# Hybrid decoder step: convolution tails transposed four chunks at a time, diagonal products regrouped by rows, sample scores of two batches together

## Chip, cores and metric

The kernel runs on one core of one Trainium2 chip. The metric is the device time of one execution in microseconds. Before the change the median of three runs is 1380.89 us (1379.9 to 1382.13).

## What is computed

One inference step of one decoder layer, for 256 prompt tokens and 8 sample requests of 4 tokens each (288 columns in all), in float32:

```python
proj = rmsnorm(x) @ w_in                       # -> z, xbc, dt, q, k, v
xbc, conv_new = causal_conv(xbc, conv0)        # width 4; conv_new = last 3 inputs per request
y, ssm_new = ssd_scan(x, dt, a, B, C, h0)      # per head: y_diag = (C B^T * decay) @ x, plus the state's part
x = x + concat(gated rmsnorm(y), sliding-window attention) @ w_out
x = x + cross_attn(rmsnorm(x), memory keys and values) # 4 heads of 128, 256 memory tokens per request
x = x + ffn(rmsnorm(x))                        # 5632 hidden units
```

The outputs are the two token streams after a last norm and all new states and caches. Among them are `conv_new` for the prompt (3 rows of 1536 channels) and for the 8 sample requests (8 times 3 rows).

## The kernel before

**Layout.** All activations stand transposed: channels on the 128 partitions, the 288 tokens along the free axis. A weight matrix is read in chunks of 128 x 1024 numbers into `raw` (3 buffers). ScalarE rounds a chunk to `hi` (line 159) and VectorE subtracts to get `lo` (line 79, called from 160 on), with 4 buffers of each; TensorE then makes three products per tile, `lo x`, `hi x` and `hi x_lo` (lines 169 to 171, named `mm`). A chunk is 24 such products of 288 columns.

**Order of the work.** The program is written as projections that follow each other. Small work is put in between by `later(n, fn)`: a heap holds functions that are emitted n chunk steps later. A scheduler then sorts the instructions of each engine by priority and by its own estimate of when an operand is ready, and each engine runs its list in that order; waits are semaphores. Weight loads have the highest priority. SyncE (SP) issues nearly all transfers.

**Convolution tails.** `conv_pair` handles two 128-channel chunks: it scales the projection (`xr`), makes four taps and the silu, and copies the last 3 prompt columns and the last 3 columns of each sample request into a tile `cc` of 27 columns. Four steps later `emit` transposes the two `cc` tiles on TensorE (two products with the identity, line 118), copies the 27 x 256 result to `co`, and SP sends two output transfers (lines 723 and 724). There are 12 chunks, so 6 pairs.

**Diagonal products.** `ssd(jj)` handles four heads. `diag` makes for each pair j of heads one PSUM tile: for the three token blocks c (128, 128 and 32 rows) and the two heads, a product of 64 output partitions (line 823). The blocks c = 0, 1 contract over 128 rows, c = 2 over 32 rows. There are four calls, jj = 0 to 3.

**Natural B.** `bc_products` transposes the B chunks (`nat_transpose`, six transposes), VectorE and ScalarE copy them out (line 745), and TensorE makes the B-C products (line 771).

**Sample scores.** In cross-attention, `sample_keys(b)` loads the keys of request b and transposes them (8 transposes), and `score` makes four products, one per head, each in its own 32 output partitions of one PSUM tile (line 1162). All eight requests accumulate into the same tile, since `qm` is zero outside the columns of its own request.

Of the kernel before, what the change touches and what calls it, by code (L numbers as in the profile page):

```python
# [8 lines left out]
F32 = mybir.dt.float32  # L9
# [3 lines left out]
ALU = mybir.AluOpType  # L13
AX = mybir.AxisListType

P = 128
D = 2048
KC = D // P
TP = 256
TS = 32  # L20
T = TP + TS
NB = 8
# [24 lines left out]
def tile_hymba_step(ctx: ExitStack, tc: tile.TileContext, I: dict, O: list, stop: int = 99):  # L47
    nc = tc.nc
# [3 lines left out]
    def tl(pool, shape, dt, tag):  # L52
        uid[0] += 1
        return pool.tile(shape, dt, name=f"{tag}_{uid[0]}", tag=tag)
# [17 lines left out]
    def psum(tag="ps"):  # L72
        return tl(p_ps, [P, 512], F32, "ps")
# [7 lines left out]
    def stt(out, in0, s, in1, op0, op1):  # L81
        nc.vector.scalar_tensor_tensor(out=out, in0=in0, scalar=s, in1=in1, op0=op0, op1=op1)  # L82
# [32 lines left out]
    def transpose(out, in_):  # L115
        k = in_.shape[0]
        b = in_.base_partition() if callable(in_.base_partition) else in_.base_partition
        nc.tensor.transpose(out, in_, ident[b:b + k, 0:k])  # L118
# [6 lines left out]
    def later(n, fn):  # L125
        uid[0] += 1
        heapq.heappush(pend, (clock[0] + n, uid[0], fn))
# [109 lines left out]
    for j, nm_ in enumerate(("sinks", "dt_bias", "a_log")):  # L237
# [4 lines left out]
    sinkb, dtb, aexp, sinkc, dsk, nsinkb, nsinkc = (  # L242
        hvec[:, a:b] for a, b in ((0, 16), (16, 32), (32, 48), (48, 50), (50, 58), (58, 74), (74, 76)))
# [78 lines left out]
    def ts(w=T, n=P, dt=F32):  # L322
        return tl(mxs, [P, 320], dt, "s")[:n, :w]
# [366 lines left out]
    conv_state()  # L690
    RW = 3 + TP + 56

    def conv_pair(c0, pcs):
        ccs = []
        for j in range(2):
            c, pc = c0 + j, pcs[j]
            xr, ac = ts(RW), ts(RW)
            smp = lambda t_: t_[:, 259:315].rearrange("p (b s) -> p b s", s=7)
            nc.gpsimd.memset(xr[:, 0:3], 0.0)
            nc.scalar.copy(smp(xr)[:, :, 0:3], scT[:, c].rearrange("p (b k) -> p b k", k=3))  # L700
            tt(nc.vector, xr[:, 3:259], pc[:, :TP], rstdb[:, :TP], ALU.mult)
            tt(nc.vector, smp(xr)[:, :, 3:7], pc[:, TP:T].rearrange("p (b t) -> p b t", t=4),
               rstdb[:, TP:T].rearrange("p (b t) -> p b t", t=4), ALU.mult)
            n = RW - 3
            act(ac[:, :n], xr[:, 0:n], AF.Identity, scale=cwT[:, c:c + 1], bias=nwcol(V_CB, c))
            for k in range(1, 4):
                stt(ac[:, :n], xr[:, k:k + n], cwT[:, 12 * k + c:12 * k + c + 1], ac[:, :n], ALU.mult, ALU.add)
            nc.gpsimd.memset(ac[:, n:], 0.0)
            act(xc[c][:, :TP], ac[:, :TP], AF.Silu)
            act(xc[c][:, TP:T].rearrange("p (b t) -> p b t", t=4), smp(ac)[:, :, 0:4], AF.Silu)  # L710
            cc = tl(mxr, [P, 27], F32, "cc")
            nc.scalar.copy(cc[:, 0:3], xr[:, 256:259])
            nc.scalar.copy(cc[:, 3:27].rearrange("p (b k) -> p b k", k=3), smp(xr)[:, :, 4:7])
            ccs.append(cc)

        def emit():
            pt = psum()
            for j in range(2):
                transpose(pt[:27, j * P:(j + 1) * P], ccs[j])
            co = ts(256)  # L720
            nc.scalar.copy(co[:27], pt[:27, 0:256])
            cs_ = slice(c0 * P, c0 * P + 256)
            nc.sync.dma_start(o_pconv[0, 0, :, cs_], co[0:3])
            nc.sync.dma_start(o_sconv[0].rearrange("b k c -> (b k) c")[:, cs_], co[3:27])

        later(4, emit)

    CH = ((0, P), (P, TP), (TP, T))
    hv_ = lambda t_: t_.rearrange("p (h d) -> p h d", d=64)
# [80 lines left out]
    def ssd(jj):  # L810
        g = jj // 2
        sgv = sgs[jj]
        *xnat, xe, xe0, xe1, xes = nat_transpose(2 * jj, 4 * jj)

        def diag():
            for j in range(2):
                i = 2 * jj + j
                ps = psum()
                for c in range(3):
                    a, b_ = CH[c]  # L820
                    for hf in range(2):
                        h4 = 2 * j + hf
                        nc.tensor.matmul(ps[64 * hf:64 * hf + 64, a:b_], xnat[c][:, 64 * h4:64 * h4 + 64],  # L823
                                         sgv[c][:, h4], start=True, stop=True)
                stt(xc[i], xc[i], dsk[:, i:i + 1], ps[:, :T], ALU.mult, ALU.add)
            x3_ = ts(256, 96, F32R)
            nc.scalar.copy(x3_[0:32], xes)
            nc.scalar.copy(x3_[64:96], xes)
            tt(nc.vector, x3_[32:64], xes, f32(x3_[0:32]), ALU.subtract)
            xs3[jj] = x3_  # L830
            later(2, states)

        def states():
            ps = psum()
            nc.tensor.matmul(ps[:, 0:256], bnat[0][:, g * P:(g + 1) * P], xe, start=True, stop=True)
            st0 = ts(256)
            nc.scalar.copy(st0, ps[:, 0:256])
            ps = psum()
            for j in range(2):
                for c, x_ in ((0, xe0), (1, xe1)):  # L840
                    nc.tensor.matmul(ps[:, j * P:(j + 1) * P], x_[:, j * P:(j + 1) * P],
                                     bnat[c][:, g * P:(g + 1) * P], start=(c == 0), stop=(c == 1))
            so = ts(256)
            nc.scalar.copy(so, ps[:, 0:256])
            nc.sync.dma_start(o_pssm[0, 0].rearrange("(k i f) p n -> k (f p) i n", k=4, f=2)[jj],
                                so.rearrange("p (i n) -> p i n", n=P))
            later(1, lambda: inter(st0))

        def inter(st0):
            ps = psum()  # L850
            for j in range(2):
                for hf in range(2):
                    h4 = 2 * j + hf
                    nc.tensor.matmul(ps[64 * hf:64 * hf + 64, j * P:(j + 1) * P], st0[:, 64 * h4:64 * h4 + 64],
                                     xc[10 + g][:, P:TP], start=True, stop=True)
            yo = ts(256)
            for j in range(2):
                i = 2 * jj + j
                tt(nc.vector, yo[:, j * P:(j + 1) * P], ps[:, j * P:(j + 1) * P], ecs[i][:, 0:P], ALU.mult)
                tt(nc.vector, xc[i][:, P:TP], xc[i][:, P:TP], yo[:, j * P:(j + 1) * P], ALU.add)  # L860
            part_done(g)

        later(1, diag)


# [249 lines left out]

    cmk, cmv = I["cache_mem_k"][0], I["cache_mem_v"][0]
    pS, pO = [], []
    pm = []

    def softmax(rows):  # L1120
# [21 lines left out]
    def sample_keys(b):  # L1142
        kk = sample_load(b, cmk)
        if not pS:
            pS.append(psum())

        def trans():
            kTb = []
            for hp in range(2):
                ps = psum()  # L1150
                for j in range(2):
                    for mc in range(2):
                        transpose(ps[:, 256 * j + P * mc:256 * j + P * mc + P],
                                  kk[mc][2 * hp + j])
                    k_ = tl(p_xb, [P, T], F32, "xb")[:, :256] if b < 2 else ts(256)
                    (nc.vector.tensor_copy if hp else nc.scalar.copy)(k_, ps[:, 256 * j:256 * j + 256])
                    kTb.append(k_)
            later(max(1, t_q + 5 - clock[0]), lambda: score(kTb))

        def score(kTb):  # L1160
            for h in range(4):
                nc.tensor.matmul(pS[0][32 * h:32 * h + 32, :TP], qm[h][:, b], kTb[h], start=(b == 0),  # L1162
                                 stop=(b == NB - 1))
            if b == NB - 1:
                sx = ts(256)
                softmax([(pS[0][:, :TP], sx, tl(lr, [P, 2], F32, "st"))])
                later(2, lambda: weights(sx))

        def weights(sx):
            ps = psum()  # L1170
            for mc in range(2):
                transpose(ps[:, mc * P:(mc + 1) * P], sx[:, mc * P:(mc + 1) * P])
                for h in range(4):
                    p_ = ts(256)
                    nc.gpsimd.memset(p_, 0.0)
                    p_ = p_.rearrange("p (b t) -> p b t", b=NB)
                    v = p_.rearrange("p b (c t) -> p (b c) t", t=4)[:, 0:64:9]
                    o0 = mc * P + h * TS
                    nc.vector.tensor_copy(v, ps[:, o0:o0 + TS].rearrange("p (b t) -> p b t", t=4))
                    pm.append(p_)  # L1180
            for b2 in range(NB):
                later(b2 // 2 + 1, lambda b2=b2: values(b2))

        later(2, trans)
# [273 lines left out]
```

## Time and profile before

| what | value |
|---|---|
| median of 3 runs | 1380.89 us |
| the profiled execution, its own time | 1382.05 us |
| its span, first to last instruction | 1380.3 us |
| TensorE busy | 1367.6 us (99%) |
| VectorE / ScalarE busy | 810.5 us (59%) / 638.4 us (46%) |
| mean transfer rate | 175 GB/s |

How to read it: "busy" counts a matmul from its start to a modelled end, and matmuls overlap in the pipeline. What a product costs in a stream is therefore the distance from its start to the start of the next row, not its duration. A row of the timeline that merges several equal instructions gives the start of the first and their count. PE is TensorE, DVE is VectorE, ACT is ScalarE. `128*27 128x128` reads: stationary operand of 128 rows and 27 columns, moving operand of 128 partitions and 128 columns.

### The profile page before, as it was taken

What the parts mean: (1) busy time and instruction counts of PE and PEld (TensorE: products, weight loads), DVE (VectorE), ACT (ScalarE), POOL (GpSimd) and SP (SyncE); (2) the same over time, 40 slices, a digit from 0 to 9 for tenths busy, and PEclk for the clock granted to TensorE, in tenths of its full rate; (3) what the DMA queues carried; (4) which work ended last, traced back from release to release, by engine and by line L of the source; (5) the groups of instructions that cost most, each with busy time, mean ns of one, the idle gap of its engine ahead of it and who ended that gap; (6) DMA issues with size and microseconds to landing.
All of it is one profiled execution on the core that took longest, in us unless ns stands there. A gap on an engine that the chain in (4) does not pass through costs nothing.

```text
span 1380.3 us, 26140 instructions
## 1 busy us (share of the span) xinstructions
PE 1367.6 (99%) x10637; PEld 1334.1 (97%) x10637; DVE 810.5 (59%) x1444; ACT 638.4 (46%) x1042; POOL 84.4 (6%) x139
## 2 busy tenths in 40 slices
PE   9999999999999999999999999999999999999997
PEld 8999999999998999999999999999999999999997
DVE  6886798876565567545545444444544544545554
ACT  7456867644454556433333333333333433434332
POOL 2010100004210122000000000000000000000110
PEclk9999999999999999999999999999999999999999
DMA  9665476588558645555555555555555555555552
GB/s 255 187 195 141 127 229 199 145 246 222 168 168 272 207 149 169 168 168 166 164 164 165 168 163 163 165 167 171 165 168 168 167 169 165 164 158 166 167 169 92
DMA packets 251392, 241.17 MB, mean 175 GB/s; under 512 B 12778, under 2 KB 242576, under 8 KB 251272
## 3 DMA queue, kind: packets, MB, share of 16 engines
q1 hardware_dynamic: 248424, 234.79, 55.7%
q0 software_dynamic: 2816, 4.70, 1.4%
q8 instruction: 83, 1.36, 0.4%
q14 instruction: 37, 0.30, 0.1%
q10 hardware_dynamic: 32, 0.01, 0.0%
HBM read 227.59 MB, written 11.85 MB: 173 GB/s over the span
## 4 chain that ended last, share of the span: by engine, by line
PE 96%; DVE 2%; ACT 1%; issue 1%; DMA 0%; POOL 0%; DVEq 0%; ACTq 0%; POOLq 0%
PE mm L169 29%; PE mm L170 29%; PE mm L171 29%; PE ps L118 3%; DVE xa L82 1%; PE ps L823 0%; DVE lo L79 0%; PE ps L521 0%; DMA xT<-xspill 0%; PE ps L1162 0%; ACT hi L159 0%; PE ps L899 0%; PE ps L1197 0%; PE ps L912 0%; PE ps L1235 0%
## 5 line engine op out<-in xcount | busy, mean ns | idle before, releaser
L79 DVE TENSOR_TENSOR lo<-raw,hi 128x1024 fp32r<-128x1024 f32 (+1 forms) x413 | 478.1, 1160 | 449.4 <-ACT hi L159 444.4
L159 ACT CAST hi<-raw 128x1024 fp32r<-128x1024 f32 (+1 forms) x413 | 410.5, 997 | 542.1 <-PE mm L171 446.7
L169 PE MATMUL mm<-xa,lo 128*128 128x288 f32 x2016 | 599.8, 298 | 0.6 <-ACT xa L174 0.6
L170 PE MATMUL mm<-xa,hi 128*128 128x288 f32 x2016 | 597.0, 296 | 0.0
L171 PE MATMUL mm<-xa,hi 128*128 128x288 f32 x2016 | 590.3, 293 | 0.0
L169 PEld LDWEIGHTS mm<-xa,lo 128*128 128x128 f32 x2016 | 378.0, 187 | 4.8 <-issue 3.1
L171 PEld LDWEIGHTS mm<-xa,hi 128*128 128x128 f32 x2016 | 379.1, 188 | 1.0 <-issue 0.7
L170 PEld LDWEIGHTS mm<-xa,hi 128*128 128x128 f32 x2016 | 378.8, 188 | 0.9 <-issue 0.3
L169 PE MATMUL mm<-ls,lo 128*128 128x288 f32 x512 | 152.4, 298 | 0.0
L171 PE MATMUL mm<-ls,hi 128*128 128x288 f32 x512 | 151.6, 296 | 0.0
L170 PE MATMUL mm<-ls,hi 128*128 128x288 f32 x512 | 151.0, 295 | 0.0
L169 PE MATMUL mm<-xb,lo 128*128 128x288 f32 x448 | 132.2, 295 | 2.9 <-DVE xT L79 2.8
L170 PE MATMUL mm<-xb,hi 128*128 128x288 f32 x448 | 132.6, 296 | 0.0
L171 PE MATMUL mm<-xb,hi 128*128 128x288 f32 x448 | 131.9, 294 | 0.0
L79 POOL TENSOR_TENSOR ssum<-ssum,ls 128x288 f32<-128x288 f32 x43 | 47.5, 1104 | 881.4 <-ACT ls L85 880.5
L170 PEld LDWEIGHTS mm<-ls,hi 128*128 128x128 f32 x512 | 96.7, 189 | 0.1
L169 PEld LDWEIGHTS mm<-ls,lo 128*128 128x128 f32 x512 | 96.6, 189 | 0.1
L171 PEld LDWEIGHTS mm<-ls,hi 128*128 128x128 f32 x512 | 96.3, 188 | 0.0
L169 PEld LDWEIGHTS mm<-xb,lo 128*128 128x128 f32 x448 | 84.6, 189 | 3.6 <-DVE xT L79 3.4
L171 PEld LDWEIGHTS mm<-xb,hi 128*128 128x128 f32 x448 | 84.6, 189 | 0.2 <-DVE xb L79 0.2
L170 PEld LDWEIGHTS mm<-xb,hi 128*128 128x128 f32 x448 | 84.0, 188 | 0.1
L79 DVE TENSOR_TENSOR xT<-xT,mm 128x288 f32<-128x288 f32 x64 | 28.2, 448 | 42.3 <-PE mm L171 37.5
(301 smaller groups left out, 1126.4 us busy)
## 6 DMA issues: line engine op xcount, KB each, us to landing
raw<-in_w_gate_dram SPq DMA_DIRECT2D x88, 512.0 KB
raw<-in_w_up_dram SPq DMA_DIRECT2D x88, 512.0 KB
raw<-in_w_down_dram SPq DMA_DIRECT2D x80, 512.0 KB
raw<-in_w_in_dram SPq DMA_DIRECT2D x43, 512.0 KB
raw<-in_w_in_dram SPq DMA_DIRECT2D x34, 256.0 KB
raw<-in_w_out_dram SPq DMA_DIRECT2D x32, 256.0 KB
raw<-in_w_out_dram SPq DMA_DIRECT2D x16, 512.0 KB
ld<-in_state_ssm_dram SPq DMA_DIRECT2D x16, 256.0 KB
```

The costliest lines, as they stand in the source:

```text
L79: eng.tensor_tensor(out=out, in0=in0, in1=in1, op=op)
L82: nc.vector.scalar_tensor_tensor(out=out, in0=in0, scalar=s, in1=in1, op0=op0, op1=op1)
L118: nc.tensor.transpose(out, in_, ident[b:b + k, 0:k])
L159: nc.scalar.copy(h_, src)
L169: nc.tensor.matmul(ps, wl, xh, start=start, stop=False)
L170: nc.tensor.matmul(ps, wh, xh, start=False, stop=False)
L171: nc.tensor.matmul(ps, wh, xl, start=False, stop=stop)
```

## The change

Three edits. (1) The tails of four chunks go into one zeroed 128 x 128 tile, 32 columns for each chunk; one transpose per four chunks takes the place of four, its copy is 128 x 128, and eight output transfers of half the row length follow it (24 in all in place of 12). (2) `diag` takes two PSUM tiles and makes the eight products of 128 rows of both head pairs first, then the four of 32 rows. (3) `score` keeps the keys of an even request and makes the products of two requests at the odd one.

```diff
+    tails = []
     def conv_pair(c0, pcs):
-        ccs = []
...
-            cc = tl(mxr, [P, 27], F32, "cc")
+            if c0 % 4 == 0 and j == 0:
+                tails.append(tl(mxr, [P, P], F32, "cc"))
+                nc.gpsimd.memset(tails[-1], 0.0)
+            cc = tails[-1][:, 32 * (c % 4):32 * (c % 4) + 27]
             nc.scalar.copy(cc[:, 0:3], xr[:, 256:259])
...
-        def emit():
-            pt = psum()
-            for j in range(2):
-                transpose(pt[:27, j * P:(j + 1) * P], ccs[j])
-            co = ts(256)
-            nc.scalar.copy(co[:27], pt[:27, 0:256])
-            cs_ = slice(c0 * P, c0 * P + 256)
-            nc.sync.dma_start(o_pconv[0, 0, :, cs_], co[0:3])
-            nc.sync.dma_start(o_sconv[0].rearrange("b k c -> (b k) c")[:, cs_], co[3:27])
-        later(4, emit)
+        def emit(cc):
+            pt = psum()
+            transpose(pt[:, 0:P], cc)
+            co = ts(P)
+            nc.scalar.copy(co, pt[:, 0:P])
+            for j in range(4):
+                cs_ = slice((c0 - 2 + j) * P, (c0 - 1 + j) * P)
+                nc.sync.dma_start(o_pconv[0, 0, :, cs_], co[32 * j:32 * j + 3])
+                nc.sync.dma_start(o_sconv[0].rearrange("b k c -> (b k) c")[:, cs_], co[32 * j + 3:32 * j + 27])
+        if c0 % 4:
+            later(4, lambda cc=tails[-1]: emit(cc))
...
         def diag():
+            pss = [psum(), psum()]
+            for j, c in ((0, 0), (0, 1), (1, 0), (1, 1), (0, 2), (1, 2)):
+                a, b_ = CH[c]
+                for hf in range(2):
+                    h4 = 2 * j + hf
+                    nc.tensor.matmul(pss[j][64 * hf:64 * hf + 64, a:b_], xnat[c][:, 64 * h4:64 * h4 + 64],
+                                     sgv[c][:, h4], start=True, stop=True)
             for j in range(2):
                 i = 2 * jj + j
-                ps = psum()
-                for c in range(3):
...
-                stt(xc[i], xc[i], dsk[:, i:i + 1], ps[:, :T], ALU.mult, ALU.add)
+                stt(xc[i], xc[i], dsk[:, i:i + 1], pss[j][:, :T], ALU.mult, ALU.add)
...
         def score(kTb):
-            for h in range(4):
-                nc.tensor.matmul(pS[0][32 * h:32 * h + 32, :TP], qm[h][:, b], kTb[h], start=(b == 0),
-                                 stop=(b == NB - 1))
+            keys2.append((b, kTb))
+            if b % 2 == 0:
+                return
+            for b2, kT2 in keys2:
+                for h in range(4):
+                    nc.tensor.matmul(pS[0][32 * h:32 * h + 32, :TP], qm[h][:, b2], kT2[h], start=(b2 == 0),
+                                     stop=(b2 == NB - 1))
+            keys2.clear()
```

The scheduler makes a new order from this, on every engine from the first tails on.

**TensorE, the diagonal products of the first four heads** (`m` and `s` on the left are the decay blocks, the `s` behind them natural x; the two `ps` numbers are the two head pairs). Before:

```order
L823 MATMUL ps_2562<-m_2034,s_2456 64x128 x2
L823 MATMUL ps_2562<-m_2035,s_2458 64x128 x2
L823 MATMUL ps_2562<-s_2036,s_2460 64x32 x2
L823 MATMUL ps_2570<-m_2034,s_2456 64x128 x2
L823 MATMUL ps_2570<-m_2035,s_2458 64x128 x2
L823 MATMUL ps_2570<-s_2036,s_2460 64x32 x2
```

Now:

```order
L825 MATMUL ps_2549<-m_2025,s_2452 64x128 x2
L825 MATMUL ps_2549<-m_2026,s_2454 64x128 x2
L825 MATMUL ps_2550<-m_2025,s_2452 64x128 x2
L825 MATMUL ps_2550<-m_2026,s_2454 64x128 x2
L825 MATMUL ps_2549<-s_2027,s_2456 64x32 x2
L825 MATMUL ps_2550<-s_2027,s_2456 64x32 x2
```

The four products of 32 rows moved behind all eight of 128 rows. This holds for jj = 0, 1, 2; the products of jj = 3 stand in four pieces between weight products as before.

**TensorE, the scores of one group** (`ls` on the left is the keys of one head, on the right `qm`; `ld` is the keys of a later request that are being transposed). Before, request 4:

```order
L118 MATMUL ps_5965<-cst,ld_5832 128x128
L118 MATMUL ps_5965<-cst,ld_5834 128x128
L1162 MATMUL ps_5578<-ls_5899,ls_5370 32x256
L1162 MATMUL ps_5578<-ls_5903,ls_5371 32x256
L1162 MATMUL ps_5578<-ls_5908,ls_5372 32x256
L1162 MATMUL ps_5578<-ls_5912,ls_5373 32x256
```

Now, requests 2 and 3:

```order
L1171 MATMUL ps_5566<-ls_5805,ls_5358 32x256
L1171 MATMUL ps_5566<-ls_5809,ls_5359 32x256
L1171 MATMUL ps_5566<-ls_5814,ls_5360 32x256
L1171 MATMUL ps_5566<-ls_5818,ls_5361 32x256
L1171 MATMUL ps_5566<-ls_5827,ls_5358 32x256
L118 MATMUL ps_5884<-cst,ld_5760 128x128
L118 MATMUL ps_5884<-cst,ld_5762 128x128
L1171 MATMUL ps_5566<-ls_5831,ls_5359 32x256
L1171 MATMUL ps_5566<-ls_5836,ls_5360 32x256
L1171 MATMUL ps_5566<-ls_5840,ls_5361 32x256
```

The eight products of a pair stand as five and three with two transposes between. Requests 0 and 1, 2 and 3, 4 and 5 all stand so; 6 and 7 stand as eight in a row. Before, requests 2 and 3 stood as five and three, 0 and 1 as four, one and three with two transposes at each cut, and 4 to 7 as four separate groups of four.

**VectorE, at the end of the first projection of x** (`lo` is a split weight chunk; the COPY reads the transposed B). Before:

```order
L79 TENSOR_TENSOR lo_2202<-raw_2200,hi_2201 128x1024
...
L79 TENSOR_TENSOR lo_2276<-raw_2274,hi_2275 128x1024
...
L79 TENSOR_TENSOR lo_2353<-raw_2351,hi_2352 128x1024
...
L799 TENSOR_SCALAR s_2036<-csb_2029,s_663 32x32 x4
L745 COPY s_2168<-ps_2160 128x256
```

Now:

```order
L803 TENSOR_SCALAR s_2027<-csb_2020,s_663 32x32 x4
...
L749 COPY s_2159<-ps_2151 128x256
L79 TENSOR_TENSOR stx_2076<-stx_2076 128x2
L624 RECIPROCAL stx_2076<-stx_2076 128x2
L626 TENSOR_SCALAR m_2074<-m_2074,stx_2076 128x144
L626 TENSOR_SCALAR m_2075<-m_2075,stx_2076 128x144
L79 TENSOR_TENSOR lo_2193<-raw_2191,hi_2192 128x1024
```

`lo_2193` is the same weight chunk as `lo_2202`, the last of that projection. Before, it and the two chunks after it were split ahead of the copy of B; now all three are split behind it. In both orders TensorE's next weight product after the B transposes and the first B-C products needs that chunk. On ScalarE, in the same place, 25 rows of other work now stand between the cast of the chunk before it and the cast `hi_2192` (before, 10 rows).

## Rows read from the trace of the kernel before

**Rows 1.** The page, busy time per engine (share, instructions).
```profile
PE 1367.6 (99%) x10637; PEld 1334.1 (97%) x10637; DVE 810.5 (59%) x1444; ACT 638.4 (46%) x1042; POOL 84.4 (6%) x139
```

**Rows 2.** Longest wait of PE: who, for whom, total us, times, longest.
```profile
PE mm L169 <- DVE xT L79: 2.8, 1, 2.8
```

**Rows 3.** Timeline of PE at one pair of tails: start, us, line, tiles, form, count.
```profile
136.68 0.29 PE L171 MATMUL mm<-xa,hi 128*128 128x288 f32 x1
136.81 0.38 PE L118 MATMUL ps<-cst,cc 128*27 128x128 f32 x2
136.95 0.38 PE L169 MATMUL mm<-xa,lo 128*128 128x288 f32 x1
137.16 0.29 PE L170 MATMUL mm<-xa,hi 128*128 128x288 f32 x1
```

**Rows 4.** Timeline of PE at the diagonal products, jj = 0 and jj = 3.
```profile
176.09 0.66 PE L823 MATMUL ps<-m,s 128*64 128x128 f32 x8
176.68 0.30 PE L823 MATMUL ps<-s,s 32*64 32x32 f32 x4
176.91 0.66 PE L823 MATMUL ps<-m,s 128*64 128x128 f32 x8
...
177.73 0.40 PE L169 MATMUL mm<-xa,lo 128*128 128x288 f32 x1
...
265.29 0.44 PE L823 MATMUL ps<-m,s 128*64 128x128 f32 x4
265.66 0.40 PE L170 MATMUL mm<-xa,hi 128*128 128x288 f32 x1
...
266.38 0.44 PE L823 MATMUL ps<-m,s 128*64 128x128 f32 x4
```

**Rows 5.** Timeline of PE at the sample scores of requests 2 to 4.
```profile
436.77 1.05 PE L1162 MATMUL ps<-ls,ls 128*32 128x256 f32 x10
437.75 0.44 PE L118 MATMUL ps<-cst,ld 128*128 128x128 f32 x2
438.12 0.63 PE L1162 MATMUL ps<-ls,ls 128*32 128x256 f32 x6
438.68 0.38 PE L169 MATMUL mm<-hi,xa 128*128 128x256 f32 x1
...
442.39 0.64 PE L1162 MATMUL ps<-ls,ls 128*32 128x256 f32 x8
442.96 0.39 PE L169 MATMUL mm<-hi,xa 128*128 128x256 f32 x1
```

**Rows 6.** Timeline of PE at the B transposes and after them.
```profile
149.87 0.82 PE L118 MATMUL ps<-cst,s 128*128 128x128 f32 x6
...
150.89 0.38 PE L169 MATMUL mm<-xa,lo 128*128 128x288 f32 x1
```

**Rows 7.** Timeline of DVE around the copy of B.
```profile
147.17 1.22 DVE L79 TENSOR_TENSOR lo<-raw,hi 128x1024 fp32r<-128x1024 f32 x1
...
150.50 0.42 DVE L745 COPY s<-ps 128x256 f32<-128x256 f32 x1 [0.54 <-PE ps L118]
152.66 0.16 DVE L79 TENSOR_TENSOR stx<-stx 128x2 f32<-128x2 f32 x1 [1.73 <-ACT stx L85]
...
153.06 0.50 DVE L626 TENSOR_SCALAR m<-m,stx 128x144 f32<-128x144 f32 x2
```

**Rows 8.** Timeline of ACT in the same stretch.
```profile
139.47 0.65 ACT L85 ACTIVATE s<-s,vT,cwT 128x312 f32<-128x312 f32 x1 [0.97 <-POOL s L699]
...
140.22 2.00 ACT L159 CAST hi<-raw 128x1024 fp32r<-128x1024 f32 x2
...
144.84 1.03 ACT L159 CAST hi<-raw 128x1024 fp32r<-128x1024 f32 x1
...
152.44 0.19 ACT L85 ACTIVATE stx<-stx 128x2 f32<-128x2 f32 x1
```

**Rows 9.** Timeline of SP, a transfer of a pair of tails.
```profile
157.05 0.28 SPq L723 DMA_DIRECT2D out_dram<-s  x1
```

More of the change, by code (lines that the diff above doesn't have):

```diff
@@ L710, in conv_pair @@
             act(xc[c][:, TP:T].rearrange("p (b t) -> p b t", t=4), smp(ac)[:, :, 0:4], AF.Silu)
-            cc = tl(mxr, [P, 27], F32, "cc")
+            if c0 % 4 == 0 and j == 0:
+                tails.append(tl(mxr, [P, P], F32, "cc"))
+                nc.gpsimd.memset(tails[-1], 0.0)
+            cc = tails[-1][:, 32 * (c % 4):32 * (c % 4) + 27]
             nc.scalar.copy(cc[:, 0:3], xr[:, 256:259])
             nc.scalar.copy(cc[:, 3:27].rearrange("p (b k) -> p b k", k=3), smp(xr)[:, :, 4:7])
-            ccs.append(cc)
-        def emit():
+        def emit(cc):
             pt = psum()
-            for j in range(2):
-                transpose(pt[:27, j * P:(j + 1) * P], ccs[j])
-            co = ts(256)
-            nc.scalar.copy(co[:27], pt[:27, 0:256])
-            cs_ = slice(c0 * P, c0 * P + 256)
-            nc.sync.dma_start(o_pconv[0, 0, :, cs_], co[0:3])
-            nc.sync.dma_start(o_sconv[0].rearrange("b k c -> (b k) c")[:, cs_], co[3:27])
-        later(4, emit)
+            transpose(pt[:, 0:P], cc)
[7 more added lines that the diff above has]
+            later(4, lambda cc=tails[-1]: emit(cc))
     CH = ((0, P), (P, TP), (TP, T))
@@ L815, in diag @@
         def diag():
+            pss = [psum(), psum()]
[5 more added lines that the diff above has]
+                                     sgv[c][:, h4], start=True, stop=True)
             for j in range(2):
                 i = 2 * jj + j
-                ps = psum()
-                for c in range(3):
[L820 to L824, printed above, removed]
-                stt(xc[i], xc[i], dsk[:, i:i + 1], ps[:, :T], ALU.mult, ALU.add)
+                stt(xc[i], xc[i], dsk[:, i:i + 1], pss[j][:, :T], ALU.mult, ALU.add)
             x3_ = ts(256, 96, F32R)
@@ L1117, in tile_hymba_step @@
     pS, pO = [], []
+    keys2 = []
     pm = []
```

## The prediction

> **What bounds the kernel now.** I read the page's engine totals first, then the waits of TensorE, then its timeline at the three places that the change edits, and last VectorE and ScalarE at the one place where the new order puts something in front of a weight product.
>
> TensorE is busy for 1367.6 of 1380.3 us, 99%, and VectorE and ScalarE for 59% and 46% [rows 1]. The longest time that TensorE waits for anything is one wait of 2.8 us, for VectorE [rows 2]. So this kernel is a queue of products, and an edit is worth what it takes out of that queue, less any new wait that it makes.
>
> The price of a product in the queue is the distance between starts. A weight product is followed after 0.13 us (136.68 to 136.81) when the stream is undisturbed, and after 0.21 us (136.95 to 137.16) when it is the first behind a pair of transposes [rows 3]. So an interruption costs its own products and about 0.08 us more at the return. Behind the diagonal products, too, four weight products come dearer: at jj = 3 the stretch between two pieces takes 266.38 - 265.66 = 0.72 us, and four at 0.13 are 0.53 us. That is 0.19 us for each cut of the weight stream [rows 4].
>
> **Part 1, the tails.** Removed: six pairs of transposes. A pair takes 136.95 - 136.81 = 0.14 us and the return 0.08 us, together 0.22 us [rows 3], six times 1.32 us. Added: three single transposes. One with 128 columns is not in the trace beside weight products; I take half the pair plus the return, 0.07 + 0.08 = 0.15 us, three times 0.45 us. Bounds: as little as the return alone (three times 0.08 us), as much as a whole pair each (three times 0.22). The saving is 1.32 - 0.45 = 0.9 us, between 0.7 and 1.1. The three clears of a tile are GpSimd's, which is busy 6% [rows 1]; ScalarE's copies become fewer. Their cover is those engines' idle time, and without it a late clear would delay only the tail's copies, which TensorE needs four steps later.
>
> *TensorEngine Tiling (Array Packing)* of the Trainium skill, Key Properties, would price this part higher: it says that a switch of tiling mode drains the array while another tile of the same mode does not. The 27-column transposes occupy a narrower tile than weight products, so by that rule each pair would pay on the way in too, and its removal would give more. The trace does not agree for them: the pair starts 0.13 us behind the weight product before it, as any weight product does [rows 3].
>
> **Part 2, the diagonal products.** A call takes 177.73 - 176.09 = 1.64 us. Its pieces: eight records (four products) of 128 rows 0.59 us, four records of 32 rows 0.23 us, and the same again [rows 4]. At jj = 3, four records of 128 rows take 265.66 - 265.29 = 0.37 us, so the second four of eight cost 0.59 - 0.37 = 0.22 us and the first four 0.15 us more, a charge at entry. In the new order the sixteen of 128 rows stand together: 0.59 + 2 x 0.22 = 1.03 us. The eight of 32 rows follow: 0.23 us for the first four, and for the second four anything from 0 to 0.23 us, since the trace shows no eight together. I take 0.16, lowered like the others by part of the entry. Sum 1.42 us, saving 0.22 us per call; bounds 0.15 and 0.38. This holds for jj = 0 to 2, 0.66 us. At jj = 2 a piece before a single weight product closes up as well, one cut less, 0.19 us. At jj = 3 the order stays in pieces, 0. Together 0.85 us.
>
> **Part 3, the scores.** The order shows how little of the edit survives: three of the four pairs still stand as five and three products with two transposes between. From the rows, a five takes 437.75 - 436.77 = 0.98 us, the two transposes 0.37 us, a three 438.68 - 438.12 = 0.56 us, and a four alone 442.96 - 442.39 = 0.57 us [rows 5]. A cut is dear: four products in one run take 0.57 us, and three almost the same, so the fixed part of a stretch is large and the transposes between them, which had to be made somewhere anyway, are not an added cost of their own. Before: one request pair cut twice (about 0.57 + 0.55 + 0.56), one as five and three (1.54 us), four alone (4 x 0.57): 5.50 us in nine stretches. Now: three times 1.54, and eight in a row at most 2 x 0.57 = 1.14 and by the step from four to five at least 0.9, say 1.0 us: 5.6 us in seven stretches. Against it stand two returns fewer and up to three more cuts of the weight stream by transposes that used to lie next to scores. I take +0.1 us, bounds -0.3 and +0.5.
>
> **What is moved.** With the tails fewer, the weight stream of the mixer has two cuts fewer beside the ones counted: 2 x 0.19 = 0.4 us, bounds 0 and 0.6, since each depends on what the scheduler puts in its place. TensorE's queue is shorter by 0.9 + 0.85 + 0.4 - 0.1, about 2.1 us.
>
> **The added wait.** On VectorE the last weight chunk of the first projection of x is now split behind the copy of the transposed B, a 128x2 sum, a reciprocal and two scalings; before, it was split ahead of them. TensorE reaches that chunk's product right behind the B transposes. Clocked from the rows of before: the transposes start at 149.87 [rows 6], VectorE's copy can start at 150.50, takes 0.42, the sum and the reciprocal 153.06 - 152.66 = 0.40, the two scalings 0.50, the split 1.22 [rows 7]. That ends at 153.04. TensorE is through the transposes and the first B-C products at 150.89 [rows 6], and a further small product that now stands there gives it some 0.2 us. So it waits from about 151.1 to 153.0, some 1.9 us. Queued behind the waiting product are all later products; nothing can be done in their place, since TensorE's list is fixed. If VectorE does the copy late, the wait grows by as much; if the scheduler's list on TensorE offers more work than I count, it shrinks to 0. Afterwards two more chunks have to be split in a row, 2 x 1.2 us, and each feeds 24 x 0.13 = 3.1 us of products, so the lag does not build up.
>
> The spec table of *TensorE: Matmul & The Clock Gate* in the Trainium skill (row on engine queues) calls the vector engines' queues strictly first in, first out. That speaks against this change: by it the split cannot pass a copy that waits for a transpose. The trace agrees as far as it goes: VectorE stood idle for 0.54 us until the copy's operand was there and started nothing from behind it [rows 7].
>
> **The cast in front of that split.** The split also needs ScalarE's rounded chunk, which now follows the 128x2 root (152.44 in before). Before, three casts stood ahead of the root, 2.00 and 1.03 us, that now stand behind it [rows 8]; so the root ends at about 152.63 - 3.03 = 149.6 and the cast at 150.6. VectorE is ready for the split at 153.04 - 1.22 = 151.8. There is slack of 1.2 us, or 2.1 if ScalarE's 0.97 us wait for GpSimd [rows 8] goes too (its zeroed tile is now cleared elsewhere in the order). So I cost the cast at nothing, with that slack as cover.
>
> **Sum.** -2.1 + 1.9 = -0.2 us on a span of 1380.3 and an own time of 1382.05: 1381.9 for such an execution. The median of the runs is 1380.89, 1.16 under the profiled one; the forecast is 1380.7 us. Measurement tells 0.2%, 2.8 us, from no change.
>
> **Rivals.** *The wait does not come.* TensorE then keeps the whole 2.1 us: 1380.89 - 2.1 = 1378.8. For it: TensorE could be behind VectorE if the earlier chunks lag. Against it: the copy of B reads the transposes themselves, so VectorE cannot be early. Chance 0.18. It stays inside 0.2% unless the unknown terms (0.2 at the tails, 0.16 x 3 at the diagonals, 0.4 at the scores) all fall well.
>
> *ScalarE's stretch starves the split.* This one ends slower. In the new order 25 rows, with five table loads, stand between two casts of weights, where before there were 10. If a projection result, a copy or a cleared tile that one of them needs comes late, the cast, the split and TensorE's product are late by that less the slack of 1.2 to 2.1 us. It decides, that is, exceeds the saving and 0.2%, when the stretch is about 3 us late beyond the slack, 5 in all; with 6 in all the time is 1380.9 - 2.1 + 1.9 + 4 = 1384.7. For it: ScalarE waits in that very stretch before, 0.97 us. Against it: a loss of 3 us would be more than any wait of TensorE in the trace [rows 2]. Chance 0.18.
>
> *SyncE is late with weights.* Eight tail transfers now stand together, each 0.28 us of its queue [rows 9], 2.2 us in place of 0.6, ahead of weight loads. If a load reaches its cast late by all of the 1.7 us, the time is 1380.7 + 1.7 = 1382.4. For it: the loads have few buffers. Against: 24 products of 0.13 us give 3.1 us per chunk, and there are four split chunks of reserve. Chance 0.12.
>
> **How the numbers follow.** The forecast has 0.52, the rivals 0.18, 0.18 and 0.12. The forecast's own terms reach from 1379 to 1382.5. Low end: the first rival with the best of the unknown terms, 1378.2. High end: between the third rival and the second, 1384.2, which leaves out part of the second. Faster by over 0.2% means below 1378.1: most of what it needs lies in the first rival with good terms, 0.14. Slower by over 0.2% means above 1383.7: the second rival and a little of the third, 0.19. The rest, 0.67, is within.
>
> **What would show it.** Tails: three single transposes of 128 columns in place of pairs of 27, with about 0.07 us each. Diagonals: one row of sixteen and one of eight records, some 1.4 us for a call. Scores: rows of ten and six records with transposes between, thrice, and one row of sixteen. The wait: a line of TensorE waiting for VectorE's split of about 1.9 us near 150 us. If that line is missing, the first rival holds; if it is over 4 us and ScalarE's cast is what ends it, the second; if a weight load ends TensorE's wait, the third. The forecast is wrong if TensorE's busy time falls by less than 1 or by more than 3.5 us.

## The result and the profile after

The changed kernel takes 1384.54 us (median of 13 runs, 1381.13 to 1385.35) against 1381.19 us of the kernel before (13 runs on the same chip, 1379.35 to 1385.26). The ratio is 1.0020 with a 95% interval of 1.0013 to 1.0027: slower by some 2.8 us; the two medians are 3.35 us apart. The forecast was 1380.7 us with a range up to 1384.2; the measured median lies above it. The profiled execution has a span of 1382.9 us, 2.6 more than before.

TensorE's busy time, from the page of the changed kernel, is up by 0.9 us against [rows 1], where a shorter queue of products was forecast. Products that run at half clock, of which more below, count in it with their longer time:

```profile
PE 1368.5 (99%) x10628; PEld 1335.9 (97%) x10628; DVE 810.3 (59%) x1444; ACT 636.4 (46%) x1039; POOL 84.6 (6%) x142
```

The waits of TensorE in the changed kernel (who, for whom, total us, times, longest). The first line answers to [rows 2]; the second and the third are new, and they are the wait that the prediction added:

```profile
PE mm L169 <- DVE xT L79: 2.4, 1, 2.4
PE mm L169 <- DVE lo L79: 1.3, 1, 1.3
...
PE ps L775 <- ACT s L749: 0.3, 1, 0.3
```

TensorE's timeline at that wait in the changed kernel (start, us, line, tiles, form, count, idle before and its releaser), which answers to [rows 6]:

```profile
149.19 0.82 PE L118 MATMUL ps<-cst,s 128*128 128x128 f32 x6
149.84 0.61 PE L775 MATMUL ps<-s,s 128*128 128x128 f32 x4
150.71 0.25 PE L775 MATMUL ps<-s,s 128*32 128x32 f32 x2 [0.26 <-ACT s L749]
152.24 0.40 PE L169 MATMUL mm<-xa,lo 128*128 128x288 f32 x1 [1.28 <-DVE lo L79]
```

VectorE and then ScalarE in the same stretch, which answer to [rows 7] and [rows 8]:

```profile
149.82 0.42 DVE L749 COPY s<-ps 128x256 f32<-128x256 f32 x1 [2.04 <-PE ps L118]
150.17 0.15 DVE L79 TENSOR_TENSOR stx<-stx 128x2 f32<-128x2 f32 x1
...
150.55 0.50 DVE L626 TENSOR_SCALAR m<-m,stx 128x144 f32<-128x144 f32 x2
150.97 1.22 DVE L79 TENSOR_TENSOR lo<-raw,hi 128x1024 fp32r<-128x1024 f32 x1
```

```profile
148.25 0.19 ACT L85 ACTIVATE stx<-stx 128x2 f32<-128x2 f32 x1
148.34 1.04 ACT L159 CAST hi<-raw 128x1024 fp32r<-128x1024 f32 x1
```

The chain is the predicted one, row for row: copy, sum, reciprocal, scalings, split. TensorE stands for 1.28 + 0.26 = 1.5 us. ScalarE's cast is done at 149.4, 1.6 us before VectorE could use it, so it had slack.

What no part of the prediction had is the clock. Windows of the kernel before (from:to, length, busy time and count per engine, granted clock, DMA share, GB/s):

```profile
160.00:180.00 20.00, 20.00 (x172) 18.04 (x171) 17.68 (x53) 15.62 (x34) 0.00 (x0) 1.00 0.60 169
320.00:340.00 20.00, 19.93 (x151) 19.70 (x150) 14.14 (x19) 10.92 (x17) 8.58 (x11) 1.00 0.85 221
```

The same of the changed kernel, with one narrower window:

```profile
160.00:180.00 20.00, 20.00 (x163) 18.36 (x162) 15.81 (x49) 15.86 (x33) 0.00 (x0) 0.91 0.65 177
320.00:340.00 20.00, 20.00 (x141) 20.00 (x141) 14.29 (x18) 10.74 (x18) 9.15 (x12) 0.91 0.85 233
...
166.00:171.00 5.00, 5.00 (x31) 4.88 (x31) 4.33 (x11) 4.38 (x6) 0.00 (x0) 0.66 0.60 158
```

The granted clock is 0.91 in each of these stretches, where before it is 1.00. By the narrower window 0.34 x 5 = 1.7 us of work are lost in the first, and the second has the same mean. Within 166 to 171 us one sees it in the weight products, which start 0.24 us apart in place of 0.13 [rows 3]:

```profile
167.00 0.44 PE L170 MATMUL mm<-xa,hi 128*128 128x288 f32 x1
167.24 0.44 PE L171 MATMUL mm<-xa,hi 128*128 128x288 f32 x1
```

This is the lower of the two levels, 1.2 in place of 2.4 GHz. TensorE was 100% busy in this window. It was idle near 150 us, then busy without a gap for 14 us, until the clock fell at 166.6 us. The second fall, at 320.2 us, comes half a microsecond after an idle time from 317.3 to 319.7 us. The Trainium skill (*TensorE: Matmul & The Clock Gate*, What's actually happening) says that the clock is set by how busy the engine has been recently; the trace agrees as far as an idle time stands ahead of both falls and products then start 0.24 in place of 0.13 us apart.

The products themselves. One tail of four chunks, jj = 0 of the diagonal products, the scores of the first pair and the end of all scores, which answer to [rows 3 to 5]:

```profile
156.26 0.29 PE L171 MATMUL mm<-xa,hi 128*128 128x288 f32 x1
156.40 0.27 PE L118 MATMUL ps<-cst,cc 128*128 128x128 f32 x1
156.42 0.38 PE L169 MATMUL mm<-xa,lo 128*128 128x288 f32 x1
156.64 0.29 PE L170 MATMUL mm<-xa,hi 128*128 128x288 f32 x1
...
178.13 1.09 PE L825 MATMUL ps<-m,s 128*64 128x128 f32 x16
179.16 0.42 PE L825 MATMUL ps<-s,s 32*64 32x32 f32 x8
179.50 0.40 PE L169 MATMUL mm<-xa,lo 128*128 128x288 f32 x1
...
428.55 0.28 PE L169 MATMUL mm<-hi,xa 128*128 128x256 f32 x1
...
432.53 0.28 PE L171 MATMUL mm<-lo,xa 128*128 128x256 f32 x1
432.87 0.44 PE L118 MATMUL ps<-cst,ld 128*128 128x128 f32 x2
...
433.50 0.28 PE L169 MATMUL mm<-hi,xa 128*128 128x256 f32 x1
433.86 1.02 PE L1171 MATMUL ps<-xb,ls 128*32 128x256 f32 x10
...
459.03 1.99 PE L1245 MATMUL ps<-ls,ls 128*128 128x256 f32 x8
```

A tail costs 0.02 us and 0.22 - 0.13 = 0.09 us at the return, together 0.11 us. A call of the diagonal products costs 179.50 - 178.13 = 1.37 us, 1.64 before. The scores are a surprise at four places: the transposes at 432.87 and the scores at 433.86 start 0.34 and 0.36 us behind a weight product that otherwise is followed after 0.12, and two more pairs of transposes, at 445.39 and 454.98 us, start 0.30 and 0.31 us behind theirs. That is 0.8 us above 0.12 each; before, no such place is in this stretch. A wait of 0.2 us is shorter than the modelled end of a product, 0.28 us, so the view of waits does not list it. Each of the three pairs of transposes starts 0.05 or 0.06 us behind the end of a copy by ScalarE, here the first; ahead of the scores a copy ends 0.15 us earlier, so their cause is less sure:

```profile
432.45 0.37 ACT L1161 COPY ls<-ps 128x256 f32<-128x256 f32 x1
```

The ends of this stretch in the kernel before, for comparison (first product of 256 columns, and the product behind the last score):

```profile
426.59 0.28 PE L169 MATMUL mm<-hi,xa 128*128 128x256 f32 x1
...
456.45 1.99 PE L1235 MATMUL ps<-ls,ls 128*128 128x256 f32 x8
```

Start times of the same work give the account by place:

| place | before | after | difference | added since the row above |
|---|---|---|---|---|
| B transposes | 149.87 | 149.19 | -0.68 | (0.43 of it before the first weight product) |
| diagonal products, jj = 0 | 176.09 | 178.13 | +2.04 | +2.72: wait 1.5, half clock 1.7, products -0.5 |
| first product of 256 columns | 426.59 | 428.55 | +1.96 | -0.08: half clock 1.7, wait near 317 us 0.4 shorter, products and the rest -1.4 |
| behind the last score | 456.45 | 459.03 | +2.58 | +0.62 |
| span | 1380.3 | 1382.9 | +2.6 | 0 |

### The profile page after: what moved, and what is told of

It is laid out like the page before. It is cut to its first block, busy times and chain, and to the rows that moved or that the text cites. A ratio compares the mean times of both kernels' runs of the same rounds, so it can differ in the third digit from the quotient of the medians.

```text
span 1382.9 us, 26129 instructions
## 1 busy us (share of the span) xinstructions
PE 1368.5 (99%) x10628; PEld 1335.9 (97%) x10628; DVE 810.3 (59%) x1444; ACT 636.4 (46%) x1039; POOL 84.6 (6%) x142
## 4 chain that ended last, share of the span: by engine, by line
PE 94%; DVE 2%; ACT 2%; issue 1%; DMA 1%; POOL 0%; DVEq 0%; ACTq 0%; SPq 0%; POOLq 0%
PE mm L169 29%; PE mm L170 28%; PE mm L171 28%; PE ps L118 3%; ACT hi L159 1%; DVE lo L79 1%; DVE xa L82 1%; PE ps L521 0%; PE ps L825 0%; PE ps L1171 0%; DMA xT<-xspill 0%; DMA raw<-in_w_in_dram 0%; PE ps L903 0%; PE ps L1207 0%; DVE xT L79 0%
```

## The experiments

Clocks are the mean granted clock that each run lists; 0.001 of it is 1.4 us. The changed kernel's own runs already speak for the clock: in its first series and in the one further down, the three runs of 24 that list 0.999 take 1381.13, 1380.84 and 1380.79 us, as much as the kernel before. So the clock does not fall in every execution of this kernel. (Two runs of other kernels list 0.946 and 0.948 without being longer, so one listed clock by itself proves little.) Two theories stood against each other from the start. A: the waits make the clock fall, and the fall is the missing term. B: the order or the products are slower, and the clock differs at random.

**The kernel before again**, unchanged.

> The unchanged kernel once more, for the granted clock of each of its runs. In the profiles so far the changed kernel has two stretches of 3.41 us at half clock (from 166.59 and from 320.19 us), the kernel before none but the one at the very end. Theory A (clock): each such stretch costs 1.7 us and explains 3.4 of the 3.35 us between the medians, so the runs of the unchanged kernel show a mean clock of 0.998 to 0.999 at 1379.5 to 1382 us, and the few slower ones a clock lower by 0.001 for each 1.7 us. Rival B (products): the changed kernel is slower by its products and waits alone, and the clock differs at random; then runs of this kernel show 0.996 about as often as those of the changed one.

Measured: 1381.74 us, ratio 1.0002 (0.9992 to 1.0012), mean clock 0.9978, where the changed kernel's 13 runs have 0.9963, a difference of 2 us. Its profile, the window that is 1.00 in the other profile of this kernel:

```profile
320.00:340.00 20.00, 20.00 (x140) 19.78 (x140) 13.02 (x17) 9.98 (x17) 7.96 (x10) 0.91 0.80 217
```

So the half clock near 320 us belongs to the kernel before too, in some executions and not in others; only that near 166 us is new. A holds so far, but the fall near 320 us, 1.7 us between the two profiles, is not the change's.

**B-C products one step later** in the changed kernel.

```diff
-    later(3, bc_products)
+    later(4, bc_products)
```

> The changed kernel with the B-C products due one chunk step later (4 in place of 3), which puts the split of the last chunk of the first x projection ahead of the copy of B again. Theory A: the wait near 150 us (1.3 and 0.3 us) goes, and with it the stretch of half clock at 166 us; the span falls from 1382.9 by 1.6 + 1.7 to about 1379.5 with a half-clock stretch near 320 us and 1378 without, median 1379 to 1381. Rival B: only the wait goes, median about 1383, the stretch at 166 us stays. Rival C (another wait takes its place, at the x transposes near 190 us): TensorE waits 1 to 2 us there and the median stays within 1 us of 1384.5.

Measured: 1382.82 us, ratio to the kernel before 1.0005 (0.9995 to 1.0014), mean clock 0.9971. The wait near 150 us and the half clock behind it are gone together; a new wait stands near 190 us (its window of 160 to 180 us, and the waits):

```profile
160.00:180.00 20.00, 19.81 (x169) 17.83 (x169) 16.95 (x51) 14.45 (x33) 0.00 (x0) 1.00 0.63 176
```

```profile
PE ps L118 <- ACT s L85: 1.0, 2, 0.8
```

A and C are both partly right: the price of the wait near 150 us goes, and 1.0 us of it comes back as another wait. The median stays above A's 1379 to 1381 us.

**Part 1 alone.** The kernel before with the first edit of the diff.

> The kernel before with part 1 alone. The order of the last split and the copy of B is then the same as in the changed kernel. Theory A: the whole loss is here: products -1.3 us (tails and cuts), wait +1.6 us, half clock near 166 us +1.7, perhaps near 320 us +1.7: median 1383 to 1385. Rival D (the regrouped products lower the clock, through their longer runs of half-filled tiles): no stretch at half clock, median about 1381.

Measured: 1384.42 us, ratio 1.0026 (1.0014 to 1.0038), mean clock 0.9952. The wait is the same, and the clock falls for twice as long (the waits, and the window):

```profile
PE mm L169 <- DVE lo L79: 1.3, 1, 1.3
```

```profile
160.00:180.00 20.00, 20.00 (x145) 18.21 (x143) 14.39 (x45) 15.45 (x30) 0.00 (x0) 0.83 0.63 173
```

Part 1 alone brings the whole loss, as A says; why the clock stays down twice as long here is open. D falls: nothing of part 2 is in this kernel.

**Part 2 alone.** The kernel before with the second edit.

> The kernel before with part 2 alone. Theory A: no wait near 150 us and no half clock near 166 us; the products save 0.85 us, median about 1380.3 against 1381.2. Rival D: half-clock stretches behind the regrouped products (after 176 us), median over 1382.

Measured: 1381.35 us, ratio 1.0001 (0.9990 to 1.0012). No half clock near 166 us:

```profile
160.00:180.00 20.00, 20.00 (x173) 18.25 (x173) 17.67 (x53) 15.55 (x34) 0.00 (x0) 1.00 0.60 170
```

By the start times of the same weight products the queue is shorter by 0.5 us at the end of the mixer, not by 0.85; too little for the runs to tell.

**Part 3 alone.** The kernel before with the third edit.

> The kernel before with part 3 alone. In the trace of the changed kernel the stretch from the first 256-column weight product of the cross-attention to the end of the scores takes 30.48 us (428.55 to 459.03), before 29.86 (426.59 to 456.45), and of that +0.62 the score products themselves are +0.1. Theory E: part 3 costs about 0.6 to 0.8 us by itself, because the weight stream is cut at other places; the stretch takes 30.4 to 30.6 us here too, everything up to 420 us is as before, and the median is 0.6 to 0.8 us above that of the kernel before. Rival F: the stretch differs because of what parts 1 and 2 do to buffers earlier; then it takes 29.9 us here.

Measured: 1380.38 us, ratio 0.9999 (0.9990 to 1.0008): the runs can't resolve it. The trace does (first product of 256 columns, and the product behind the last score):

```profile
426.71 0.28 PE L169 MATMUL mm<-hi,xa 128*128 128x256 f32 x1
...
457.19 1.99 PE L1241 MATMUL ps<-ls,ls 128*128 128x256 f32 x8
```

457.19 - 426.71 = 30.48 us, as in the changed kernel, against 29.86 before, and the same four places are late. The stretch takes 30.48 us in all five profiles with part 3 and 29.86 in all nine without it. E holds: part 3 costs 0.6 us by itself.

**The wait near 150 us filled** in the changed kernel, beside the changed kernel again on the same chip.

```diff
     def bc_products():
...
+        pf = psum()
+        with tc.high_priority(offset=0):
+            for _ in range(16):
+                nc.tensor.matmul(pf[:, 0:P], xc[8][:, 0:P], xc[10][:, 0:P], start=True, stop=True)
```

> The changed kernel once more, to stand beside the next one on the same chip. Theory A: most runs at a clock of 0.995 to 0.997 (mean 0.996), 2 to 3.5 us above the runs of the kernel before, and a half-clock stretch between 160 and 170 us in the profile.

> The changed kernel with 16 products of 128 columns more, whose result nobody reads, between the B transposes and the weight product that waits for its split near 150 us; the split itself stands where it stood, so the weight product cannot start before 152.2 us. The order also puts the last three B-C products ahead of it, which may leave one wait of up to 1 us. Theory A (idle time brings the half clock): no half-clock stretch between 155 and 200 us, mean clock of the runs 0.001 above after_again, time 0 to 2 us below it although 1.7 us of useless products were added. Rival B (the half clock comes with the order or the products, not with the idle time): the stretch near 165 us stays and the time is equal or higher.

Measured: the changed kernel again 1382.42 us, ratio 1.0006 (0.9997 to 1.0016), so only 0.8 us above the kernel before where 2 to 3.5 were expected; mean clock 0.9965, and in its profile the same two windows at 0.91. Filled: 1383.96 us, ratio 1.0027 (1.0015 to 1.0039), mean clock 0.9972. The window, and TensorE's timeline:

```profile
160.00:180.00 20.00, 20.00 (x178) 18.51 (x177) 17.10 (x52) 16.87 (x36) 0.00 (x0) 1.00 0.80 229
```

```profile
149.26 0.82 PE L118 MATMUL ps<-cst,s 128*128 128x128 f32 x6
...
150.36 1.73 PE L771 MATMUL ps<-s,s 128*128 128x128 f32 x14
...
178.47 1.09 PE L829 MATMUL ps<-m,s 128*64 128x128 f32 x16
```

The price of the filling was mis-sized: a product has two records of 0.11 us, so sixteen are 3.6 us and not 1.7, and the forecast of the time was wrong. The mechanism is shown all the same. The split is as late as in the changed kernel, though TensorE's list is not quite the same: the last B-C products now stand ahead of the waiting weight product. TensorE is never idle there, and the half clock does not come in this profile: with 3.6 us of useless products the diagonal products start at 178.47, only 0.34 us later than in the changed kernel. B falls. Among the twelve runs three still list 0.995 or 0.996, so it is not gone from every execution.

**The wait near 317 us filled** in the kernel before, first with too much.

```diff
+            if mp_ == 2:
+                pf = psum()
+                for _ in range(28):
+                    nc.tensor.matmul(pf[:, 0:P], ident, ident, start=True, stop=True)
             pss = gemm(att_chunks(c0) + kchunks(w_out, 8, c0, 256), KC, 2, mix)
```

> The kernel before with 28 products of the identity by the identity, whose result nobody reads, that stand where TensorE waits: 7 of them in its wait near 309 us (in place of 8 transposes that move behind) and 21, some 2.3 us, in the wait of 2.8 us near 316 us. Theory A (the clock falls because TensorE stood idle shortly before): the half-clock stretch near 318 to 320 us, which the profiles of three of four kernels without any change near there show, does not come; runs have a clock of 0.998 or more and the median falls by 0.5 to 1.5 us, since the wait itself stays filled and not shortened. Rival G (the clock falls whatever TensorE does there, or because of the work, not of the idle time): the stretch stays, median equal or up to 0.5 us above.

Measured: 1381.39 us, ratio 0.9995 (0.9985 to 1.0005). All eleven runs have a clock of 0.998 or 0.999, mean 0.9984 against 0.9976 of the kernel before beside them, and the window of its profile is at 1.00:

```profile
320.00:340.00 20.00, 20.00 (x154) 20.00 (x153) 8.92 (x11) 7.19 (x10) 7.37 (x8) 1.00 0.71 205
```

The clock is as A says; the time is not, since the products took some 2 us more than the wait. Over all fourteen profiles, the clock falls near 320 us in nine of the ten that leave this wait unfilled (the first profile of the kernel before is the tenth) and in none of the four that fill it.

**The same wait filled to measure.** 20 products of 0.12 us, placed so that they push existing work into the wait:

```diff
         def emit(k):
...
+            if cp == 0 and k == 3:
+                xf = ymx[7][1]
+                with tc.high_priority(offset=600):
+                    for _ in range(20):
+                        nc.tensor.matmul(ps[:, TP:2 * TP], xf[:, 0:P], xf[:, 0:TP], start=True, stop=True)
```

> The kernel before with 20 products of 256 columns whose result nobody reads, 20 times 0.12 = 2.4 us, put some 25 weight products ahead of the wait of 2.8 us near 317 us; every other product keeps its place. (The 28 products of before_filled took 6.2 us by its trace, two records each, and pushed 8 transposes behind: they filled the wait and 2 us more.) Theory A: the wait shrinks to 0.2 to 0.5 us, no half clock near 320 us, so the runs have 0.998 or 0.999 and the mean time falls by the 1 to 1.7 us that the half clock took on average: 1379.5 to 1380.5. Rival G: the useless work costs what it takes or nothing, the clock stays at a mean of 0.9977, time equal.

Measured: 1376.45 us (5 runs, 1375.78 to 1378.65) against 1381.87 (9 runs, 1380.87 to 1383.0): ratio 0.9964 (0.9950 to 0.9977), mean clock 0.9986 against 0.9977. This kernel beats both. Its timeline, and its window:

```profile
312.28 2.55 PE L1084 MATMUL ps<-xa 128*128 128x256 f32 x20
...
318.54 0.40 PE L169 MATMUL mm<-xb,lo 128*128 128x288 f32 x1 [0.27 <-DVE xT L79]
```

```profile
320.00:340.00 20.00, 20.00 (x154) 20.00 (x153) 14.30 (x16) 10.39 (x18) 8.22 (x10) 1.00 0.82 209
```

The clock explains 0.0009 x 1380 = 1.2 us of the gain of 5.4. The trace bears that out: the first product of 256 columns, here and then in the second profile of the kernel before, where the clock falls, is 1.6 us apart:

```profile
425.82 0.28 PE L169 MATMUL mm<-hi,xa 128*128 128x256 f32 x1
```

```profile
427.45 0.28 PE L169 MATMUL mm<-hi,xa 128*128 128x256 f32 x1
```

The rest is more than A expected and is not shown to come from the filling; the profiled execution, 1378.65 us, is the slowest of the five. What its profile shows of the rest stands in the last section.

**Parts 1 and 2 without the wait**, and the same with either filling. The B-C products are due after 4 steps, the tails after 2, and part 3 is left off:

```diff
-    later(3, bc_products)
+    later(4, bc_products)
...
-            later(4, lambda cc=tails[-1]: emit(cc))
+            later(2, lambda cc=tails[-1]: emit(cc))
```

> Parts 1 and 2 without part 3, with the B-C products due after 4 steps in place of 3 and the tails due after 2 steps in place of 4, so that the wait near 150 us does not come and the x transposes near 190 us are not held up by ScalarE. Theory A with E: products -0.95 (tails) and -0.5 (diagonals) and no new wait over 0.7 us before 300 us, no half clock at 165 us: median 1.5 us below the kernel before, 1379 to 1380 us. Rival C: a wait of 1 us or more stands elsewhere between 150 and 300 us, and the median is that of the kernel before.

> The kernel of td_moved with the same 28 products of the identity near 309 and 316 us. Theory A: 0.5 to 1.5 us below td_moved, clocks of 0.998 and 0.999 in nearly all runs. Rival G: as td_moved or slower.

> Parts 1 and 2 with the later B-C products and earlier tails (as td_moved), with the same 20 products. Theory A: 1 to 1.5 us below before_fit by the shorter queue of products (by the trace of td_moved, -1.2 us by 300 us), with a mean clock of 0.998 or more: 1378.5 to 1379.5, the fastest of all, if a wait of 0.6 to 0.9 us for a load near 210 us does not eat it. Rival C: that wait takes the gain, time as before_fit.

Measured: 1381.6 us, ratio 1.0002 (0.9993 to 1.0010), without filling; 1380.85 us, 0.9996 (0.9987 to 1.0005), with the 28 products; 1377.53 us, 0.9968 (0.9956 to 0.9981), with the 20. The first two are inconclusive; the first is not the 1379 to 1380 us that A expected. In its profile the wait near 317 us has grown to 3.3 us, from 2.8 and 2.5 in the two of the kernel before, and the clock falls for twice as long: part of what is saved ahead of that wait is lost in it. The third is faster than the kernel before but not than the filled kernel before: the shorter queue of parts 1 and 2 (about 1 us by 300 us) is not seen in the runs. In its profile 0.8 us of it is left at the first product of 256 columns (425.00 against 425.82), although a wait for a load has grown to more than was feared:

```profile
PE ps L118 <- DMA ld<-in_state_ssm_dram: 1.3, 1, 1.3
```

## Why the prediction was wrong

**What bounds the kernel, parts 1 and 2: right, part 2 too large.** Tails: forecast -0.9, by rows 3 x 0.11 in place of 6 x 0.22, -1.0 us. Diagonal products: forecast 1.42 us a call, measured 1.37, but over the mixer -0.5 in place of -0.85 us. With the two cuts, forecast -2.15 in all; the places of the account give -0.25, -0.5 and part of -1.4. The second profiles of both kernels compare better, since the clock falls near 320 us in each. There the first product of 256 columns starts 1.2 us later with the change, at 428.65 against 427.45 us:

```profile
428.65 0.28 PE L169 MATMUL mm<-hi,xa 128*128 128x256 f32 x1
```

The wait and the half clock behind it are 1.5 + 1.7 us of that, and the changed kernel had started its stream 0.2 us earlier, so the products saved some 1.8 us.

**Part 3: mis-sized.** Forecast +0.1 (bounds -0.3 and +0.5), measured +0.6. The score products themselves came out as summed. What was missing are four hidden waits of 0.2 us, together 0.8, three of them where transposes reach TensorE before ScalarE's copy is done; the sentence that took "up to three more cuts" as balanced by fewer returns is the one that failed.

**The added wait: right in place and cause, 1.5 us in place of 1.9.** VectorE's list was read correctly; TensorE came 0.7 us earlier and so did the chain.

**The sum: this step failed.** "-2.1 + 1.9 = -0.2 us" priced a wait at its length and put what the clock does after it at nothing. The wait of 1.5 us near 150 us brings a stretch at half clock some 14 us later that costs 1.7 us more, in the profiles of both kernels that have the wait unfilled (the changed one twice), and in none of the others. That is shown from both sides: taken out with the wait (B-C products later), and taken out with the wait's place kept (filled). With it the change's own account is 1.5 + 1.7 + 0.6 - 1.8 = +2.0 us in place of -0.2; the spans of the second profiles, 1378.7 and 1380.6 us, are 1.9 apart. The runs gave +2.8 us (1.0020) on one chip and +0.8 (1.0006, 0.9997 to 1.0016) on another, so the size is less sure than the mechanism.

**The rivals.** *The wait does not come*: no, it came. *ScalarE's stretch starves the split*: its sign and nearly its result came true (1384.7 forecast for it), but by coincidence; its mechanism did not, since the cast was early by 1.6 us. *SyncE is late with weights*: the eight transfers stand together as said, from 157.09 to 161.00 us, with one weight load among them. No weight load ends a wait of TensorE in the changed kernel, so it cost nothing.

## What to carry to other kernels

Where TensorE is 99% busy, price a new idle time on it at its length plus what the clock takes back afterwards: here 1.5 us of waiting cost 1.5 + 1.7. Read the granted clock by windows behind every wait before reading anything else, since a span that grew with no longer wait to show for it may have grown there. An unavoidable wait can be filled with useless products, if they are no longer than it: 20 that fitted went with 1376.45 against 1381.87 us, of which the trace explains 1.6 us, and 28 that were too long gave nothing.

## What the runs showed that was not expected

Weight products in the same program run at two paces over long stretches, at a granted clock of 1.00 in both. The windows of two executions of the kernel before, the first profile and the second:

```profile
600.00:700.00 100.00, 100.00 (x759) 100.00 (x758) 50.79 (x64) 39.50 (x48) 0.00 (x0) 1.00 0.54 168
```

```profile
600.00:700.00 100.00, 100.00 (x765) 100.00 (x764) 51.31 (x64) 39.42 (x48) 0.00 (x0) 1.00 0.55 169
```

759 and 765 products in 100 us: 132 and 131 ns each, over some 280 us about 2.3 us. The profile of before and the first of after are at the slow pace there; the second profile of either kernel is at the fast one. Of the ten profiles that leave the wait near 317 us unfilled, six have a fast stretch from about 530 to 815 us and four have none; in all four filled variants it lies near 950 to 1230 us. What sets it stays open. It is as large as the change, it hides effects of 1 us in the runs, and it may be part of the 5 us by which the kernel filled to measure beats the one before; how much of that gain would last over more than its five runs was not tried.
